# A decoder layer on one core: two streams of matrix work paced by VectorE's load, probabilities scaled on ScalarE, block loads spread, and 24 low parts subtracted by accumulating DMAs

## The chip, the core and the metric

The kernel runs on one core of a Trainium2 chip. The metric is device time in microseconds (us) of one launch; lower is better. TensorE (PE) multiplies, VectorE (DVE), ScalarE (ACT) and GpSimd (POOL) do element work, SyncE (SP) issues transfers, and 16 DMA engines carry them. Each engine works through its own list of instructions in order.

## The reference

One decoder layer on 256 tokens of width 2048, all in fp32: three gated branches, merged by sigmoid gates, an output projection and a LayerNorm.

```python
q_a, k_a, v_a, z_a, u_g, v_g, z_g, q_c, z_c, g_logit = split(x @ w_in)     # 9 x 1024 and 3 x 2048 channels
y_a = causal_attention(q_a, k_a, v_a) * silu(z_a)        # 8 heads of 128; 256 tokens are one block
y_g = spatial_gating(u_g, v_g) * silu(z_g)               # gelu, LayerNorm of v, 128x128 causal mixing, 8 groups
y_c = attention(q_c, mem @ w_mem_k, mem @ w_mem_v) * silu(z_c)   # 4 heads of 256, 256 memory tokens
merged = g0 * (y_a @ w_branch_attn) + g1 * (y_g @ w_branch_sgu) + g2 * (y_c @ w_branch_mem)   # g = sigmoid(g_logit)
out = layer_norm(alpha * x + merged @ w_out)
```

## The kernel before, in words

**Products in parts.** Each fp32 operand is cut into a high part `hi`, the value rounded by a ScalarE copy, and a low part `lo = v - hi`, a VectorE subtraction (`split`, lines 58 to 60). A product is three passes on TensorE: hi by hi, hi by lo, lo by hi.

**Two streams.** TensorE works on two lists of steps that are woven into each other.
- A *c-step* (`classic`) uses one half, 128x1024, of a weight chunk of 1 MB. `load_chunk` loads a chunk into `raw` (two buffers, a third early on), `prep_half` splits a half into `hi` and `lo` (three buffers each, so a new half takes the buffers of the half three before it), two halves ahead of the one in use. Most c-steps make a tile of 128 channels, with 8 matmuls of 512 columns (line 187) and 8 of 256 (line 188); those of a branch projection have 12 of 512 (lines 719 to 721). The chunks in order: memory values 0 to 7 (`mv`), memory keys 8 to 15 (`mk`), `zc` 16 to 23, `qc` 24 to 31, `za` 32 to 34, memory branch 35 to 42, `za` 43 to 47, `qk` 48 to 63 (queries and keys of the attention, which runs beside them), `ug` 64 to 66, attention branch 67 to 74, `ug` 75 to 79, `zg` 80 to 87 (with the mixing of branch B beside it), gating branch 88 to 95, output 96 to 111.
- An *s-step* (`s_stream`) is one half of a product of a Strassen-Winograd scheme with 7 products in a unit; 8 units make 112 steps. Six units make the gate logits, two make `v_a` and `v_g`. A step has 12 matmuls of 512 columns (lines 391 to 393). It needs the parts `sh` (ScalarE) and `sl` (VectorE) of a 128x2048 block, four buffers for both kinds, which the memory tokens `memhl0` to `memhl3` occupy until the memory keys are done. For 64 steps VectorE first subtracts two blocks (lines 309 and 322). The blocks `b0` to `b3` (B11, B12, B22, B21) are loaded by `s_load` into the buffers `rA` and `rB`; sums of x (`xf`) are made early, stored in DRAM and loaded again.

**The order.** The c-steps and s-steps are written out in one order, s-steps at an even rate (`C_STEPS`, `LEAD`, `TAIL` at the end of the code). A scheduler then orders each engine's instructions by its own estimate of when they are ready. All DMAs are issued by SP, in order; `tc.issue_after` chains the early loads so that one is issued after the other has landed, and `riders` are loads tied behind a chunk's load.

**Attention.** Line 594 (attention over tokens, 16 times) and line 534 (over the memory, 8 times) multiply a block of exponentials by the reciprocals of their sums, on VectorE.

Of the kernel before, what the change touches and what calls it, by code (L numbers as in the profile page):

```python
# [27 lines left out]
def decoder_layer(ctx, tc, xT, memT, x_tok, w_st, w_mv, w_mk, w_zc, w_qc, w_za, w_qk, w_ug, w_zg,  # L28
# [63 lines left out]

    def load_chunk(i):

        if 0 < i < 16:
            with tc.issue_after(loaded[i - 1].ins):
                load_one(i)
        else:
            load_one(i)
        for fn in riders.pop(i, ()):  # L100
            with tc.issue_after(loaded[i].ins):
                fn()
# [30 lines left out]
    def prep_half():  # L133
        i, h = divmod(ptr["half"], 2)
        ptr["half"] += 1
        if i in held_at:
            hi, lo = held_at[i](h)
            split(hi, lo, raw[i][:, h].rearrange("p (k c) -> p k c", c=S))
        else:
            hi = wts.tile([P, 1024], F32R, tag="hi", name=f"hi{i}_{h}", bufs=3)  # L140
            lo = wts.tile([P, 1024], F32R, tag="lo", name=f"lo{i}_{h}", bufs=3)
            n = 512 if i == 0 else 1024
            for c in range(0, 1024, n):
                split(hi[:, c:c + n], lo[:, c:c + n], raw[i][:, h, c:c + n])
# [100 lines left out]
    def x_stages():  # L245

        X, F = {}, {}

        def load(g):
            def go():  # L250
                X[g] = wts.tile([P, 2, 4, S], F32, tag="rB", name=f"X{g}", bufs=4)
                nc.sync.dma_start(X[g], xT_v[g])
            return go

        def parts(g, f):
            return lambda: split(xhl_v[g][:, f, :, 0:S], xhl_v[g][:, f, :, S:2 * S], X[g][:, f])

        def sums(g):
            def go():
                F[g] = wts.tile([P, 4, 4, P], F32, tag="rA", name=f"F{g}", bufs=2)  # L260
                a11, a12 = (X[g][:, f, :, 0:P] for f in range(2))
                a21, a22 = (X[g][:, f, :, P:S] for f in range(2))
                s1, s2, s3, s4 = (F[g][:, i] for i in range(4))
                nc.vector.tensor_tensor(s1, a21, a22, op=ALU.add)
                nc.vector.tensor_tensor(s2, s1, a11, op=ALU.subtract)
                nc.vector.tensor_tensor(s3, a11, a21, op=ALU.subtract)
                nc.vector.tensor_tensor(s4, a12, s2, op=ALU.subtract)
            return go

        def sum_parts(g, i):  # L270
            def go():
                t = wts.tile([P, 4, 2 * P], F32R, tag="xsf", name=f"xw{g}{i}", bufs=3)
                split(t[:, :, 0:P], t[:, :, P:2 * P], F[g][:, i])
                late.append(lambda: nc.sync.dma_start(xf_d[i + 1, g], t.bitcast(F32)))
            return go

        return ([load(0), load(1)], [fn for g in range(2) for fn in
                                     [parts(g, 0), parts(g, 1), sums(g)] + [sum_parts(g, i) for i in range(4)]])
# [32 lines left out]
    def s_prep(s):  # L311
# [22 lines left out]
            s_load(u + 1, B11, h)  # L334
        elif p == "M2":
            s_load(u + 1, B22, h)

    def snap(name):
        return work.tile([P, 512], F32, tag="snap", name=name, bufs=5)

    def s_stream(finish):

# [117 lines left out]
            step(go)  # L460
            yield

    riders[5], riders[6] = [x_loads[0]], [x_loads[1]]
    for _ in run(mem_values()):
        pass
    for i, _ in enumerate(run(mem_keys())):
        if x_work:
            x_work.pop(0)()
        if i in (2, 4):
            with tc.issue_after(loaded[ptr["load"] - 1].ins):  # L470
                s_load(0, B12, i // 2 - 1)
        if i in (10, 12):
            for blk in (B11, B22):
                with tc.issue_after(loaded[ptr["load"] - 1].ins):
                    s_load(0, blk, i // 2 - 5)
# [31 lines left out]
    def mem_head(h, q):  # L507
        st = {}

        def fetch():  # L510
            st["k"] = w2(f"mkh{h}", (P, 2, S))
            st["v"] = w2(f"mvh{h}", (P, 2, S))
            for kk in range(2):
                nc.sync.dma_start(st["k"][:, kk], mk_d[2 * h + kk])
            for t in range(2):
                nc.sync.dma_start(st["v"][:, t], mv_d[t, h // 2][:, (h % 2) * S:(h % 2 + 1) * S])

        def scores():
# [13 lines left out]
            nc.vector.reciprocal(sm, sm)  # L532
            for t in range(2):
                nc.vector.tensor_scalar(p[:, t], p[:, t], sm[:, t:t + 1], None, op0=ALU.mult)
            st["p"] = p

        def transposes():
            ps = new_aux(f"mpt{h}", (P, 2, S))
            for mi in range(2):
                for t in range(2):  # L540
                    nc.tensor.transpose(ps[:, mi, t * P:(t + 1) * P], st["p"][:, t, mi * P:(mi + 1) * P], ident)
            st["pt"] = w2(f"mptT{h}", (P, 2, S))
            nc.scalar.activation(st["pt"], ps, AF.Copy)
# [32 lines left out]
    def moba_head(h, q, k):  # L576
        st = {}

        def scores():
# [11 lines left out]
                                     accum_out=sm[:, i:i + 1])  # L591
            nc.vector.reciprocal(sm, sm)
            for i, sl in enumerate((slice(0, P), slice(P, 384))):
                nc.vector.tensor_scalar(p[:, sl], p[:, sl], sm[:, i:i + 1], None, op0=ALU.mult)
            st["p"] = p
            st["v"], st["z"] = w1(f"vah{h}", (P, 2, P)), w1(f"sza{h}")
            for t in range(2):
# [181 lines left out]
        yield from gating()  # L779
        yield from gated_branch(1, 2)  # L780

    C_STEPS, S_STEPS = 160, 14 * UNITS
    LEAD, TAIL = 5, 11
    cs, ss = classic(), s_stream(s_finish)
    done_c = done_s = 0
    for _ in run(cs):
        done_c += 1
        while done_s < S_STEPS and done_s * (C_STEPS - LEAD - TAIL) < (done_c - LEAD) * S_STEPS:
            step(lambda: next(ss))
            done_s += 1  # L790
    flush()


# [129 lines left out]
```

## Time and profile before

| | |
|---|---|
| median of 3 runs | 1005.45 us (1003.4 to 1006.7) |
| profiled execution | 1006.0 us |
| its span, first to last instruction | 1004.3 us |
| granted clock, mean over the span | 0.994 of full speed |
| TensorE idle in the span | 24.8 us |

The page gives the busy time of each engine, then groups of instructions; the trace behind it gives the same for any stretch. The stages stand at these times: memory values to 55 us, memory keys to 99, `zc` and the first s-steps from there, `qk` with the attention 426 to 594, the attention branch 650 to 725, `zg` with the mixing 763 to 846, the gating branch 846 to 901.

### The profile page before, as it was taken

Reading aid. Unit: us, or ns where it says so; the run is one execution under the profiler, and the core shown is the slowest. Engines: PE = TensorE matmul, PEld = TensorE weight load, DVE = VectorE, ACT = ScalarE, POOL = GpSimd, SP = SyncE. Lnnn points to the kernel's source line nnn. Section 1 sums busy time; section 2 is a strip of 40 time slices with the busy share of each in tenths; the row PEclk is TensorE's granted clock in tenths of the full one; section 3 lists DMA queues with packets and bytes.
Section 4 is the critical chain, followed back from the end, with each engine's and each line's share of the span. In section 5 each row is a group of like instructions: output and inputs, shape, how many; then the busy total and the mean of one; then the engine's idle time right before and its main releaser. Section 6 shows DMA issues by size and latency. Waiting matters only on the chain.

```text
span 1004.3 us, 12911 instructions
## 1 busy us (share of the span) xinstructions
PE 979.5 (98%) x4888; PEld 824.4 (82%) x4888; DVE 819.6 (82%) x800; ACT 590.5 (59%) x647; POOL 13.2 (1%) x17
## 2 busy tenths in 40 slices
PE   9999899999999999999999999998999999999995
PEld 7788788888888888888888888876888888878885
DVE  5875986698769987978998898889998989676647
ACT  5744555565586556556566557696566558445520
POOL 0000000000000000000000000000000002000000
PEclk9999999999999999999999999999999999999998
DMA  8899578946896599379548945995899477668622
GB/s 322 315 365 419 217 252 308 338 141 228 316 333 222 218 390 354 132 288 373 219 147 312 359 150 207 340 343 186 303 371 372 143 293 256 247 234 319 227 83 84
DMA packets 68125, 269.28 MB, mean 268 GB/s; under 512 B 7520, under 2 KB 21600, under 8 KB 45536
## 3 DMA queue, kind: packets, MB, share of 16 engines
q1 hardware_dynamic: 68064, 268.47, 72.5%
q8 instruction: 38, 0.62, 0.2%
q14 instruction: 23, 0.19, 0.0%
HBM read 245.37 MB, written 23.07 MB: 267 GB/s over the span
## 4 chain that ended last, share of the span: by engine, by line
PE 79%; DVE 9%; DMA 6%; issue 3%; ACT 3%; SPq 0%; DVEq 0%; ACTq 0%
PE sM L391 8%; PE sM L392 8%; PE sM L393 8%; PE za L187 3%; PE k L187 3%; PE q L187 3%; PE zg L187 3%; PE qc L187 3%; PE mk L187 3%; PE mv L429 3%; PE o L806 3%; PE o L807 3%; PE o L805 3%; PE zc L187 3%; PE b L720 2%
## 5 line engine op out<-in xcount | busy, mean ns | idle before, releaser
L59 ACT ACTIVATE hi<-raw 128x1024 fp32r<-128x1024 f32 (+1 forms) x218 | 228.3, 1050 | 220.7 <-PE b L721 35.5
L60 DVE TENSOR_TENSOR lo<-raw,hi 128x1024 fp32r<-128x1024 f32 (+1 forms) x218 | 262.4, 1209 | 77.4 <-ACT hi L59 73.6
L60 DVE TENSOR_TENSOR sl<-b,sh 128x2048 fp32r<-128x2048 f32 x112 | 255.7, 2285 | 48.3 <-ACT sh L59 48.1
L59 ACT ACTIVATE sh<-b 128x2048 fp32r<-128x2048 f32 x112 | 214.3, 1913 | 85.1 <-PE sM L392 79.6
L309 DVE TENSOR_TENSOR b<-b,b 128x2048 f32<-128x2048 f32 x48 | 109.5, 2283 | 15.3 <-DMA b<-in_w_st_dram 15.3
L391 PE MATMUL sM<-sh,xf 128*128 128x512 f32 x256 | 100.8, 394 | 2.8 <-ACT sh L59 2.8
L392 PE MATMUL sM<-sl,xf 128*128 128x512 f32 x256 | 100.7, 393 | 2.6 <-DVE sl L60 2.6
L393 PE MATMUL sM<-sh,xf 128*128 128x512 f32 x256 | 100.6, 393 | 0.0
L391 PE MATMUL sM<-sh,xhl 128*128 128x512 f32 x192 | 76.4, 398 | 1.6 <-ACT sh L59 1.6
L720 PE MATMUL b<-lo,yhl 128*128 128x512 f32 x192 | 75.6, 394 | 1.8 <-DVE lo L60 1.6
L393 PE MATMUL sM<-sh,xhl 128*128 128x512 f32 x192 | 75.9, 395 | 0.0
L392 PE MATMUL sM<-sl,xhl 128*128 128x512 f32 x192 | 75.8, 395 | 0.0
L721 PE MATMUL b<-hi,yhl 128*128 128x512 f32 x192 | 73.7, 390 | 0.0
L719 PE MATMUL b<-hi,yhl 128*128 128x512 f32 x192 | 73.3, 394 | 0.3 <-ACT hi L59 0.2
L391 PEld LDWEIGHTS sM<-sh,xf 128*128 128x128 f32 x256 | 48.1, 188 | 13.8 <-ACT sh L59 3.3
L392 PEld LDWEIGHTS sM<-sl,xf 128*128 128x128 f32 x256 | 48.2, 188 | 12.6 <-DVE sl L60 3.0
L393 PEld LDWEIGHTS sM<-sh,xf 128*128 128x128 f32 x256 | 48.1, 188 | 10.1
L187 PE MATMUL k<-xhl,hi 128*128 128x512 f32 x128 | 46.8, 403 | 0.0
L187 PE MATMUL za<-xhl,hi 128*128 128x512 f32 x128 | 46.2, 400 | 0.0
L187 PE MATMUL q<-xhl,hi 128*128 128x512 f32 x128 | 46.2, 399 | 0.0
L187 PE MATMUL ug<-xhl,hi 128*128 128x512 f32 x128 | 45.9, 398 | 0.2 <-ACT hi L59 0.2
L187 PE MATMUL zc<-xhl,hi 128*128 128x512 f32 x128 | 45.6, 399 | 0.5 <-ACT hi L59 0.4
(297 smaller groups left out, 1889.8 us busy)
## 6 DMA issues: line engine op xcount, KB each, us to landing
b<-in_w_st_dram SPq DMA_DIRECT2D x64, 1024.0 KB, 7.3
xf<-xf SPq DMA_DIRECT2D x64, 512.0 KB, 5.6
raw<-in_w_br_dram SPq DMA_DIRECT2D x24, 1024.0 KB, 6.5
raw<-in_w_qk_dram SPq DMA_DIRECT2D x16, 1024.0 KB, 7.1
raw<-in_w_o_dram SPq DMA_DIRECT2D x16, 1024.0 KB, 4.8
raw<-in_w_mk_dram SPq DMA_DIRECT2D x8, 1024.0 KB, 9.9
raw<-in_w_zc_dram SPq DMA_DIRECT2D x8, 1024.0 KB, 7.1
raw<-in_w_qc_dram SPq DMA_DIRECT2D x8, 1024.0 KB, 6.6
```

The source lines that it names most:

```text
L59: nc.scalar.activation(hi, v, AF.Copy)
L60: nc.vector.tensor_tensor(lo, v, hi.bitcast(F32), op=ALU.subtract)
L187: nc.tensor.matmul(ps, hi, x, start=first, stop=False)
L309: nc.vector.tensor_tensor(o, rt[u, other, h], o, op=ALU.subtract)
L391: nc.tensor.matmul(ps, ah, hi[:, c], start=first, stop=False, skip_group_check=True)
L392: nc.tensor.matmul(ps, ah, lo[:, c], start=False, stop=False, skip_group_check=True)
L393: nc.tensor.matmul(ps, al, hi[:, c], start=False, stop=last, skip_group_check=True)
L429: nc.tensor.matmul(ps[t][n], lhs, rhs[:, n * 512:(n + 1) * 512], start=(k == 0 and rhs is hi and lhs is xh[t]), stop=(k == KT - 1 and lhs ...
L719: nc.tensor.matmul(ps[t], yh, hi[:, c], start=(k == 0), stop=False)
L720: nc.tensor.matmul(ps[t], yh, lo[:, c], start=False, stop=False)
L721: nc.tensor.matmul(ps[t], yl, hi[:, c], start=False, stop=(k == 7))
L805: nc.tensor.matmul(ps[:, 0:n], mh, hi, start=first, stop=False)
```

## The change

1. The even rate of the s-steps is replaced by a plan (`pace`): each kind of c-step has a cost in VectorE time, an s-step costs 3.2, and s-steps are put where the running sum leaves room, with due times by which a unit's results must stand. The s-steps in the stretch of each kind of chunk go, from before to after: `zc` 9 to 11, `qc` 12 to 8, `za` 5 to 6, memory branch 11 to 12, `za` 8 to 8, `qk` 26 to 32, `ug` 3 to 6, attention branch 15.0 to 14.8, `ug` 7 to 6, `zg` 13 to 8, gating branch 3 to 0.
2. The scaling of the probabilities goes from VectorE to ScalarE (24 instructions).
3. For the second half of the chunks 48 to 63 and 80 to 87, 24 halves, the low part is no longer a VectorE subtraction: ScalarE writes -hi into `lo` and GpSimd issues a DMA that adds `raw` to it (128x1024, 512 KB).
4. The first blocks' loads are spread over earlier chunks as riders, the sums of x move from `rA` to the buffers `snap`, and the chain of loads runs to chunk 19 instead of 15.

```diff
+            if h == 1 and i in by_dma:
+                nc.scalar.activation(lo, raw[i][:, h], AF.Copy, scale=-1.0)
+                nc.gpsimd.dma_start(lo.bitcast(F32), raw[i][:, h], accum_op=ALU.add)
+                nc.scalar.activation(hi, raw[i][:, h], AF.Copy)
+            else:
+                for c in range(0, 1024, n):
+                    split(hi[:, c:c + n], lo[:, c:c + n], raw[i][:, h, c:c + n])
...
+    by_dma = list(range(len(chunks), len(chunks) + 16))
     chunks += [w_qk[j] for j in range(16)]
...
+    by_dma += list(range(len(chunks), len(chunks) + 8))
     chunks += [w_zg[j] for j in range(8)]
...
-                F[g] = wts.tile([P, 4, 4, P], F32, tag="rA", name=f"F{g}", bufs=2)
+                F[g] = [snap(f"F{g}{i}", (P, 4, P)) for i in range(4)]
...
-    riders[5], riders[6] = [x_loads[0]], [x_loads[1]]
+    riders.update({4: [x_loads[0]], 5: [first(B12, 0)], 6: [x_loads[1]], 7: [first(B12, 1)],
+                   10: [first(B11, 0)], 12: [first(B11, 1)]})
...
-                nc.vector.tensor_scalar(p[:, t], p[:, t], sm[:, t:t + 1], None, op0=ALU.mult)
+                nc.scalar.activation(p[:, t], p[:, t], AF.Copy, scale=sm[:, t:t + 1])
...
-        while done_s < S_STEPS and done_s * (C_STEPS - LEAD - TAIL) < (done_c - LEAD) * S_STEPS:
+        for _ in range(plan[i] if i < len(plan) else 0):
```

ScalarE between the memory keys and `zc`, before. `sh0` and `sh1` are the high parts of the first two s-steps, `hi16` those of the first `zc` chunk, `mk7l` and `zc0l` copies of finished tiles:

```order
L59 ACTIVATE hi16_0_865<-raw16_723 128x1024
L59 ACTIVATE hi16_1_890<-raw16_723 128x1024
L59 ACTIVATE sh0_917<-b0_0_0_775 128x2048
L207 ACTIVATE mk7l_914<-mk7_864 128x256
L207 ACTIVATE zc0l_1060<-zc0_994 128x256
L59 ACTIVATE sh1_921<-b0_0_1_833 128x2048
```

The same place after:

```order
L62 ACTIVATE sh0_923<-b0_0_0_418 128x2048
L62 ACTIVATE hi16_0_869<-raw16_730 128x1024
L62 ACTIVATE hi16_1_894<-raw16_730 128x1024
L62 ACTIVATE sh1_927<-b0_0_1_505 128x2048
L218 ACTIVATE mk7l_920<-mk7_868 128x256
L62 ACTIVATE hi17_0_1001<-raw17_843 128x1024
L62 ACTIVATE sh2_1135<-b0_0_0_418 128x2048
L62 ACTIVATE hi17_1_1022<-raw17_843 128x1024
L218 ACTIVATE zc0l_1066<-zc0_1000 128x256
```

`sh1` stood behind `zc0l`, which waits for the first `zc` tile; it and `sh2` now stand ahead of it.

SP beside the end of the memory values, before (`X1` is the second half of x, `xw` are sums of x on their way to DRAM, `b` a block):

```order
L252 DMA X1_266<-in_xT_dram 128x2x1024
L120 DMA mraw7_303<-in_memT_dram 128x512
L122 DMA raw7_302<-in_w_mv_dram 128x2048
L122 DMA raw8_340<-in_w_mk_dram 128x2048
L274 DMA xf1_0_97<-xw00_576 128x1024
```

and after:

```order
L263 DMA X1_268<-in_xT_dram 128x2x1024
L123 DMA mraw7_305<-in_memT_dram 128x512
L125 DMA raw7_304<-in_w_mv_dram 128x2048
L306 DMA b1_0_1_308<-in_w_st_dram 128x2048
L285 DMA xf1_0_97<-xw00_585 128x1024
L285 DMA xf2_0_99<-xw01_614 128x1024
L285 DMA xf3_0_101<-xw02_641 128x1024
L125 DMA raw8_344<-in_w_mk_dram 128x2048
```

A block's load and three stores now stand ahead of the load of chunk 8.

ScalarE near the end of `qk`, where chunk 62 is prepared, before:

```order
L59 ACTIVATE hi62_0_4800<-raw62_4637 128x1024
L207 ACTIVATE q6l_4770<-q6_4687 128x256
L59 ACTIVATE sh68_4764<-b3_4_0_4442 128x2048
L59 ACTIVATE hi62_1_4820<-raw62_4637 128x1024
L606 ACTIVATE ptT4_4682<-pt4_4678 128x384
L59 ACTIVATE hi63_0_4872<-raw63_4730 128x1024
```

and after:

```order
L62 ACTIVATE hi62_0_4955<-raw62_4794 128x1024
L611 ACTIVATE ptT4_4838<-pt4_4834 128x384
L150 ACTIVATE hi62_1_4998<-raw62_4794 128x1024
L62 ACTIVATE sh74_4881<-b0_5_0_4470 128x2048
L148 ACTIVATE lo62_1_4999<-raw62_4794 128x1024
L62 ACTIVATE hi63_0_5054<-raw63_4890 128x1024
```

`lo62_1`, on VectorE's list before, is now a ScalarE copy, here with `sh74` between it and its high part; the accumulating DMA on GpSimd's list waits for it.

## Rows read from the trace of the kernel before

**Rows 1.** The page's first part: busy us of each engine, share, instructions.

```profile
PE 979.5 (98%) x4888; PEld 824.4 (82%) x4888; DVE 819.6 (82%) x800; ACT 590.5 (59%) x647; POOL 13.2 (1%) x17
```

**Rows 2.** Stretches: length; busy PE, PEld, DVE, ACT, POOL; clock, DMA share, GB/s.

```profile
40.00:55.00 15.00, 13.51 (x60) 10.73 (x59) 15.00 (x20) 9.70 (x12) 0.00 (x0) 1.00 0.85 287
55.00:99.30 44.30, 44.30 (x258) 38.73 (x257) 25.25 (x28) 22.17 (x27) 0.00 (x0) 1.00 1.02 412
99.30:126.00 26.70, 23.47 (x111) 19.08 (x110) 24.88 (x15) 14.34 (x14) 0.00 (x0) 0.94 0.60 223
426.00:594.00 168.00, 168.00 (x875) 142.95 (x874) 143.54 (x140) 99.55 (x119) 0.00 (x0) 1.00 0.73 271
650.00:725.00 75.00, 70.15 (x310) 55.79 (x308) 69.99 (x70) 53.53 (x53) 0.00 (x0) 1.00 0.77 278
762.60:846.00 83.40, 83.40 (x437) 71.11 (x436) 76.07 (x71) 55.70 (x57) 10.13 (x7) 1.00 0.70 259
846.00:901.40 55.40, 53.98 (x253) 44.29 (x252) 40.32 (x52) 28.93 (x38) 1.57 (x1) 1.00 0.67 238
```

**Rows 3.** Waits, 650 to 725 us: total us, times, longest.

```profile
PE sM L392 <- DVE sl L60: 2.6, 1, 2.6
```

**Rows 4.** Timeline 104 to 116 us: start, length, [idle before <-releaser].

```profile
104.47 0.40 PE L187 MATMUL zc<-xhl,hi 128*128 128x512 f32 x1
104.82 0.39 PE L391 MATMUL sM<-sh,xhl 128*128 128x512 f32 x1
...
105.02 0.38 ACT L207 ACTIVATE zc0l<-zc 128x256 f32<-128x256 f32 x1 [5.16 <-PE zc L188]
105.30 1.91 ACT L59 ACTIVATE sh<-b 128x2048 fp32r<-128x2048 f32 x1
...
108.84 1.89 ACT L59 ACTIVATE sh<-b 128x2048 fp32r<-128x2048 f32 x1
...
110.79 0.50 PE L391 MATMUL sM<-sh,xf 128*128 128x512 f32 x1 [2.83 <-ACT sh L59]
...
111.82 0.57 PE L392 MATMUL sM<-sl,xhl 128*128 128x512 f32 x1
...
115.17 0.45 PE L392 MATMUL sM<-sl,xf 128*128 128x512 f32 x1
```

**Rows 5.** Groups by line and shape: count, busy us, mean ns, idle before.

```profile
L60 DVE TENSOR_TENSOR lo<-raw,hi 128x1024 fp32r<-128x1024 f32 x214 | 259.7, 1219 | 74.6 <-ACT hi L59 70.8 <-PE sM L392 2.5 <-PE q L188 0.3
L60 DVE TENSOR_TENSOR sl<-b,sh 128x2048 fp32r<-128x2048 f32 x112 | 255.7, 2285 | 48.3 <-ACT sh L59 48.1
L59 ACT ACTIVATE hi<-raw 128x1024 fp32r<-128x1024 f32 x214 | 225.8, 1058 | 217.9 <-PE b L721 35.5 <-PE o L807 30.8 <-PE zc L187 14.7
L59 ACT ACTIVATE sh<-b 128x2048 fp32r<-128x2048 f32 x112 | 214.3, 1913 | 85.1 <-PE sM L392 79.6 <-DVE b L309 3.3 <-DMA raw<-in_w_za_dram 1.5
L309 DVE TENSOR_TENSOR b<-b,b 128x2048 f32<-128x2048 f32 x48 | 109.5, 2283 | 15.3 <-DMA b<-in_w_st_dram 15.3
L594 DVE TENSOR_SCALAR p<-p,sm 128x256 f32<-128x256 f32 x8 | 2.8, 347 | 0.0
L711 ACT ACT_TABLE_LOAD x9 | 11.5, 1283 | 3.2 <-DMA sg<-gl 3.1
```

**Rows 6.** DMA issues: count, KB each, median us from issue to landing.

```profile
xf<-xf SPq DMA_DIRECT2D x64, 512.0 KB, 5.6
raw<-in_w_qk_dram SPq DMA_DIRECT2D x16, 1024.0 KB, 7.1
raw<-in_w_mk_dram SPq DMA_DIRECT2D x8, 1024.0 KB, 9.9
raw<-in_w_zg_dram SPq DMA_DIRECT2D x7, 1024.0 KB, 6.5
```

**Rows 7.** GpSimd in the `zg` stretch, from the timeline.

```profile
777.65 2.42 POOL L664 TENSOR_SCALAR_AFFINE_SELECT ws<-ws 128x128 f32<-128x128 f32 x1 [10.70 <-ACT hi L59]
784.94 0.29 POOL L664 TENSOR_SCALAR_AFFINE_SELECT ws<-ws 128x128 f32<-128x128 f32 x1 [4.87 <-DMA ws<-in_w_sT_dram]
```

More of the change, by code (lines that the diff above doesn't have):

```diff
@@ L43, in w2, with snap @@
         return work.tile(list(shape), F32, tag="w2", name=name, bufs=6)
+    def snap(name, shape=(P, 512)):
+        return work.tile(list(shape), F32, tag="snap", name=name, bufs=5)
     def spill(name, shape, dt=F32):
@@ L93, in load_chunk @@
     def load_chunk(i):
-        if 0 < i < 16:
+        if 0 < i < 20:
             with tc.issue_after(loaded[i - 1].ins):
@@ L142, in prep_half @@
             n = 512 if i == 0 else 1024
-            for c in range(0, 1024, n):
-                split(hi[:, c:c + n], lo[:, c:c + n], raw[i][:, h, c:c + n])
+            if h == 1 and i in by_dma:
[5 more added lines that the diff above has]
+                    split(hi[:, c:c + n], lo[:, c:c + n], raw[i][:, h, c:c + n])
             ready.append((hi, lo))
@@ L259, in go @@
             def go():
-                F[g] = wts.tile([P, 4, 4, P], F32, tag="rA", name=f"F{g}", bufs=2)
+                F[g] = [snap(f"F{g}{i}", (P, 4, P)) for i in range(4)]
                 a11, a12 = (X[g][:, f, :, 0:P] for f in range(2))
                 a21, a22 = (X[g][:, f, :, P:S] for f in range(2))
-                s1, s2, s3, s4 = (F[g][:, i] for i in range(4))
+                s1, s2, s3, s4 = F[g]
                 nc.vector.tensor_tensor(s1, a21, a22, op=ALU.add)
@@ L272, in go @@
                 t = wts.tile([P, 4, 2 * P], F32R, tag="xsf", name=f"xw{g}{i}", bufs=3)
-                split(t[:, :, 0:P], t[:, :, P:2 * P], F[g][:, i])
+                split(t[:, :, 0:P], t[:, :, P:2 * P], F[g][i])
                 late.append(lambda: nc.sync.dma_start(xf_d[i + 1, g], t.bitcast(F32)))
@@ L336, in s_prep @@
             s_load(u + 1, B22, h)
-    def snap(name):
-        return work.tile([P, 512], F32, tag="snap", name=name, bufs=5)
     def s_stream(finish):
@@ L461, in run @@
             yield
-    riders[5], riders[6] = [x_loads[0]], [x_loads[1]]
+    first = lambda blk, h: lambda: s_load(0, blk, h)
+    riders.update({4: [x_loads[0]], 5: [first(B12, 0)], 6: [x_loads[1]], 7: [first(B12, 1)],
+                   10: [first(B11, 0)], 12: [first(B11, 1)]})
     for _ in run(mem_values()):
@@ L468, in decoder_layer @@
             x_work.pop(0)()
[L469 to L475, printed above, removed]
+        if i in (12, 14):
+            riders[ptr["load"]] = [first(B22, i // 2 - 6)]
     while x_work:
@@ L593, in scores @@
             for i, sl in enumerate((slice(0, P), slice(P, 384))):
-                nc.vector.tensor_scalar(p[:, sl], p[:, sl], sm[:, i:i + 1], None, op0=ALU.mult)
+                nc.scalar.activation(p[:, sl], p[:, sl], AF.Copy, scale=sm[:, i:i + 1])
             st["p"] = p
@@ L780, in classic, with pace @@
         yield from gated_branch(1, 2)
-    C_STEPS, S_STEPS = 160, 14 * UNITS
-    LEAD, TAIL = 5, 11
+    S_STEPS = 14 * UNITS
+    KINDS = ([(16, 1.2), (16, 1.75), (6, 1.2), (16, 1.3), (10, 1.2), (32, 1.15), (6, 1.2), (16, 1.6), (10, 1.2),
+              (16, 1.7), (16, 1.9)])
+    C_COST = [cost for n, cost in KINDS for _ in range(n)]
+    DUE = {38: 14, 46: 28, 64: 42, 102: 56, 110: 70, 126: 84, 144: 98, 152: 112}
+    S_COST = 3.2
+    def pace(share):
+        plan, busy, time, s = [], 0.0, 0.0, 0
+        for i, cost in enumerate(C_COST):
+            busy, time, n = busy + cost, time + 2.35, 0
+            lag = max(busy - share * time, -2.0)
+            busy = share * time + lag
+            while i >= 4 and s < S_STEPS and n < 2 and (busy + S_COST <= share * (time + 2.25) or
+                                                        any(i + 3 >= at and s < due for at, due in DUE.items())):
+                busy, time, s, n = busy + S_COST, time + 2.25, s + 1, n + 1
+            plan.append(n)
+        return plan, s
+    share = 0.80
+    while pace(share)[1] < S_STEPS or sum(pace(share)[0][:148]) < S_STEPS:
+        share += 0.005
+    plan = pace(share)[0]
     cs, ss = classic(), s_stream(s_finish)
-    done_c = done_s = 0
-    for _ in run(cs):
-        done_c += 1
-        while done_s < S_STEPS and done_s * (C_STEPS - LEAD - TAIL) < (done_c - LEAD) * S_STEPS:
+    for i, _ in enumerate(run(cs)):
+        for _ in range(plan[i] if i < len(plan) else 0):
             step(lambda: next(ss))
-            done_s += 1
     flush()
```

## The prediction, made before the changed kernel ran

> **What bounds the kernel now.** I read the page's busy times first. TensorE works 979.5 us, VectorE 819.6, ScalarE 590.5 [rows 1]. With 24.8 us of idle time TensorE is the bound: a change that takes nothing from its list can win little more than that, plus what slow matmuls cost. So the next question is where TensorE idles, and the busy time by stretch tells it [rows 2]. At the end of the memory values, 40 to 55 us, it loses 1.5 us, and VectorE is busy without a break. From 99.3 to 126, where the first s-steps start, it loses 3.2 and the clock is 0.94. In the attention branch, 650 to 725, it loses 4.9, VectorE being busy 69.99 of 75. In the gating branch, 846 to 901, it loses 1.4. The rest lies at the program's two ends. In `qk` (168.00 of 168) and in `zg` (83.40 of 83.40) it loses nothing. The reader is to see that the largest single edit, the 24 low parts, falls in the two stretches where TensorE waits for nobody. The waits show who holds it in the attention branch: a low part on VectorE, 2.6 us at once [rows 3]. The timeline shows the start: `sh1` is late, because ScalarE's list has `zc0l` ahead of it, and that waits 5.16 us for the first `zc` tile [rows 4].
>
> **What leaves VectorE.** 24 low parts at 1.219 are 29.3 us, and 24 scalings at 0.347 or somewhat less (the narrow ones are half as wide) about 8, together 37 of 819.6 [rows 1, 5]. Where they leave, they free nothing that TensorE waited for. They pay only through the plan: `qk` takes about 6 s-steps more, so `zg` takes 5 and the gating branch 3 fewer. But neither had much to win (0 and 1.4 us of idle), and the attention branch, which did wait for VectorE, keeps its 15 steps and its own low parts. I take 0 for this; the bounds are 0 and −6.3 (all that these two branches lose).
>
> ScalarE gets 24 more copies at 1.058, 25.4 us, and about 10 for the scalings. In `qk` it is busy 99.55 of 168, and with six more s-steps (six `sh` at 1.913) the sum stays near three quarters of a stretch that grows by 16 us. TensorE's work hides this; without the cover a late copy would cost up to its own microsecond.
>
> **T1, the first s-steps.** Before, TensorE waits 2.83 us for `sh1` and comes back slow: eight matmuls from 111.82 to 115.17, 3.35 us [rows 4]. The usual spacing is 44.30 / (129 + 129/2) = 0.23 for 512 columns, since half the 258 matmuls of the memory keys have 256 [rows 2]. The eight lose 3.35 − 8 x 0.23 = 1.5. At 0.42 each they ran near half speed, the lower level of 1.2 GHz, after the engine had idled; the stretch's granted clock of 0.94 agrees. Together 4.3 us. Afterwards `sh1` is ahead of `zc0l`, and the order puts the first s-step directly behind the memory keys. Its `sh0` gets a buffer when the first half of the last key chunk is done, one half (44.30 / 16 = 2.8 us) before the end. 1.91 for `sh0` and 2.28 for `sl0` end 1.4 after that end; a matmul on either side of the change of stream covers 0.46. So 0.9 is the new wait. For the second step VectorE has `sl0`, two low parts of `zc`, a block subtraction and `sl1` in a row: 2.28 + 2.44 + 2.28 + 2.28 = 9.3, ending 8.4 after the end of the keys; it is wanted at 0.9 + 2.8 + 5.6 = 9.3. It fits with 0.9 to spare. T1 = −4.3 + 0.9 = −3.4, bounds −4.3 and 0.
>
> **T2, the memory values.** SP now has a block of 1 MB and three stores ahead of chunk 8. The stretch moved 287 GB/s where the next one moves 412 [rows 2]: room for 15 x 125 KB/us = 1.9 MB. The two blocks come out of the memory keys, so those are relieved. x comes a chunk earlier, which spreads VectorE's work of that stretch. Bounds −1.5 (its whole idle time) and +2.5 (1 MB at 412 GB/s in series); I take a third of the gain, −0.5, since VectorE had no gap there.
>
> **T3, the attention branch.** ScalarE changes its function table 10 times between chunks 67 and 74 in the old order and 5 times in the new, 1.283 each [rows 5]. The scaling on ScalarE joins the exponentials without a change. ScalarE is not the late one here (53.53 of 75), so of 6.4 us I take 1.0: T3 = −1.0, bounds 0 and −4.9.
>
> **T4, the accumulating DMAs.** The trace has none. What counts is the lead: the time from the last use of the old low part in a buffer to the first use of the new. ScalarE's two copies take 2.1 of it, the transfer D the rest. I counted TensorE's list between the two and priced it at 0.23 and 0.115. Chunk 84: 28 matmuls of 512, 16 of 256 and four small mixing ones, 8.8 us; chunk 85 the same; chunk 48: 8.6; chunk 62: 8.8. There `sh74` stands between the two copies; the high part starts 0.6 earlier, so the copies end 3.4 after the buffer is free. Next come 87 (10.0), 86 (11.1), 49 (11.3), 56, 63 and 80 (11.4), 50 (11.5), 55 (11.8), the others 12.1 to 17.8. D is bounded below by the 512 KB loads, 5.6, and above by 1 MB in a crowded queue, 9.9; a DMA that reads two times 512 KB is nearest to the 1 MB loads of these stretches, 6.5 in `zg` and 7.1 in `qk` [rows 6]. I take 6.5: all leads hold but chunk 62's, 6.5 + 3.4 − 8.8 = 1.1. At 5.6 that is 0.2. At 7.1 it is 0.6 + 1.7 + 0.4 + 0.4 = 3.1. At 9.9 twelve are late and the sum is 20.4.
> The raw buffer is held through the DMA as well: load 6.5, high part 1.06, copies 2.1, DMA 6.5 make 16.2 for a buffer, against about 17.4 in which TensorE does two `zg` chunks (four halves at 2.8, two s-steps at 2.7, mixing). That fits by 1.2. Behind the held load on SP stand the next `xf` loads, wanted two s-steps later (about 11 us against 5.6), and blocks. On GpSimd the accumulates wait behind the affine selects of the mixing weights, ahead of chunks 82, 84 and 86.
>
> The Trainium skill, page "DMA: Bandwidth & Descriptors", section "Anatomy of one DMA — SWDGE (gpsimd) path", gives about 2.0 us plus bytes at 436 GB/s, by which 1 MB would take an estimated 4.4; no accumulate would be late and the sum below would end 1.1 lower. No run so far shows such a transfer.
>
> **Sum.** On the profiled execution (1006.0, of which the span is 1004.3): −3.4 − 0.5 − 1.0 + 1.1 = −3.8, so 1002.2. The profiled run stands 0.6 over the median 1005.45; on the median the forecast is 1001.6.
>
> **Rival 1, the accumulates come late (slower).** Place: TensorE before a `lo` matmul of chunks 48, 62, 84 to 87. The gains, T1 to T3, are 4.9, so within the 0.3% (3 us) that a measurement can tell from no change, it decides from T4 = 7.9, at D = 8.2. GpSimd may be held up: the same affine select took 0.29 and 2.42 us, with VectorE busy nearly throughout [rows 2, 7]. Such a hold-up before each DMA gives D = 8.9 and T4 = 11.3; with 9.9 it is 20.4; halfway, 9.4, about 15, and 1005.45 − 4.9 + 15 = 1015.5. Against it: the sources lie on the chip, and DMA shares are 0.73 and 0.70.
> The Trainium skill, page "SBUF — State Buffer", section "SBUF: two separate sides", states that VectorE and GpSimd share a port pair as an exclusive lock. A VectorE operation with two inputs there shuts out only a GpSimd operation that reads the memory too, and only VectorE's two-port modes keep GpSimd from writing a DMA's descriptors. The affine select's extra 2.1 us agrees with the first half. By the second, the subtractions here wouldn't hold up the accumulates and the sum stays; if they do, it is this rival.
>
> **Rival 2, the relief reaches TensorE.** If all waits behind VectorE and ScalarE go, 1.5 + 4.9 + 1.4 and the start's 3.2 + 1.5 leave: −12.5, 993. For it: VectorE is the releaser in the attention branch, and 37 us less work lets it run ahead before it gets there. Against: leads are capped by three `lo` buffers and four for `sh` and `sl`, so it can't store an advance; and that stretch keeps its load.
>
> **Rival 3, the start gains nothing.** The `zc` stretch has VectorE busy 24.88 of 26.70 already, and takes two s-steps more; if the 0.9 to spare is not there, VectorE sets the pace and T1 is 0. With T2 0 and T3, T4 as above this is 1005.5.
>
> **How the numbers follow.** Forecast 0.42, own range 997 to 1006 (T1 to T4 at nearer bounds); of it faster 0.25, same 0.15, slower 0.02. Rival 1 0.25, between 1007 and 1021; same 0.03, slower 0.22. Rival 2 0.21, all faster. Rival 3 0.12; same 0.10, slower 0.02. That makes faster 0.46, same 0.28, slower 0.26. The range reaches into rival 2 to 991 and into rival 1 to 1017, leaving some 0.06 below and 0.09 above.
>
> **What would show it.** T1: no wait of 5 us on ScalarE before the first `zc` copy, full clock from 99 to 126, a wait near 0.9 for `sl0`. T3: TensorE's wait for VectorE in the attention branch stays at 3 to 5 us. T4: the landing time of the GpSimd DMAs near 6.5 and one wait of TensorE, at chunk 62; `qk` and `zg` else full. Landing times over 8.2, or many waits for a DMA at `lo` matmuls, make the forecast wrong; so does a new wait behind ScalarE in `qk`, or an attention branch that closes its gap.

## The result and the profile after

The changed kernel takes 1015.04 us (median of 4 runs, 1012.25 to 1017.34) against 1005.06 for the kernel before (4 runs): a ratio of 1.0103, 95% interval 1.0083 to 1.0122. It is 10 us slower. The forecast was 1001.6; the time came out where Rival 1 had it (1015.5).

The profiled execution is the fastest of the four (1012.25, span 1010.5), so its trace shows some 6 of the 10 us. The first part of its page, then what the page says of the new DMAs (queue: packets, MB, share of 16 engines; issues: count, KB each, median us to landing):

```profile
PE 979.4 (97%) x4888; PEld 822.7 (81%) x4888; DVE 788.9 (78%) x752; ACT 617.5 (61%) x695; POOL 28.0 (3%) x41
...
q0 software_dynamic: 3456, 12.58, 6.5%
...
lo<-raw POOLq DMA_DIRECT2D x24, 512.0 KB, 7.4
raw<-in_w_mk_dram SPq DMA_DIRECT2D x8, 1024.0 KB, 9.4
```

VectorE lost 31 us of busy time, where the prediction took 37 off its list, and TensorE has the same work as before [rows 1]. The stretches of the same stages (columns as in [rows 2]): end of the memory values, first s-steps, `qk`, attention branch, `ug`, `zg`, gating branch.

```profile
35.00:55.00 20.00, 17.23 (x74) 13.29 (x73) 17.29 (x21) 11.72 (x15) 0.00 (x0) 1.00 1.01 383
99.80:126.00 26.20, 26.20 (x138) 22.32 (x137) 26.20 (x18) 16.55 (x18) 0.00 (x0) 1.00 0.52 201
421.00:610.00 189.00, 185.19 (x947) 156.24 (x946) 146.28 (x123) 129.23 (x153) 12.83 (x15) 1.00 0.94 304
646.70:733.20 86.50, 85.25 (x380) 70.30 (x378) 82.40 (x71) 58.99 (x60) 0.00 (x0) 1.00 0.81 309
733.20:781.00 47.80, 46.17 (x236) 38.22 (x234) 46.90 (x43) 29.88 (x30) 0.25 (x1) 1.00 0.71 242
781.00:860.40 79.40, 72.46 (x381) 60.98 (x380) 43.45 (x55) 51.70 (x61) 12.13 (x15) 0.98 0.87 253
860.40:907.30 46.90, 45.61 (x214) 36.80 (x213) 33.04 (x45) 27.07 (x35) 0.28 (x1) 1.00 0.79 285
```

Read length minus PE. The first s-steps lost 3.2 us before and nothing now; the attention branch 4.9 before and 1.3 now. `qk` and `zg`, which had no idle time at all [rows 2], now lose 3.8 and 6.9. In `zg` VectorE is busy 43 of 79 us: it is not short of VectorE. The waits of TensorE name who came last (total us, times, longest):

```profile
PE zg L199 <- DMA lo<-raw: 4.7, 3, 2.9
PE q L199 <- DMA lo<-raw: 3.2, 3, 1.5
PE zg L198 <- ACT hi L62: 2.3, 2, 1.8
...
PE mk L198 <- ACT hi L62: 1.6, 1, 1.6
...
PE mk L199 <- DVE lo L63: 0.8, 1, 0.8
```

Six of the 24 accumulating DMAs land after TensorE wants them, 7.9 us in sum. The two waits in the memory keys (`mk`) are new too, and make up most of the 2.8 us that the first row above loses: chunk 8 comes late behind the block and the stores that now stand ahead of it. Its load takes 10.9 us from issue to landing, and took 6.0 before. One late accumulate in the timeline, the first:

```profile
417.94 0.99 POOL L149 DMA_DIRECT2D lo<-raw  x1 [415.76 <-DVE za L219]
...
423.76 0.28 PE L199 MATMUL q<-xhl,lo 128*128 128x256 f32 x1
423.88 0.40 PE L198 MATMUL q<-xhl,hi 128*128 128x512 f32 x1
425.28 0.39 PE L199 MATMUL q<-xhl,lo 128*128 128x256 f32 x1 [1.00 <-DMA lo<-raw]
```

It landed 7.3 us after its issue; TensorE stood with the old half done and the new low part not there. The longest of the six waits, 2.9 us at chunk 84, came about in another way:

```profile
816.95 1.06 ACT L62 ACTIVATE hi<-raw 128x1024 fp32r<-128x1024 f32 x1 [1.21 <-DMA raw<-in_w_zg_dram]
...
819.17 1.04 ACT L148 ACTIVATE lo<-raw 128x1024 fp32r<-128x1024 f32 x1
820.13 1.83 POOL L669 TENSOR_SCALAR_AFFINE_SELECT ws<-ws 128x128 f32<-128x128 f32 x1 [8.14 <-DMA ws<-in_w_sT_dram]
821.90 0.85 POOL L149 DMA_DIRECT2D lo<-raw  x1
...
824.50 0.40 PE L198 MATMUL zg<-xhl,hi 128*128 128x512 f32 x1
824.85 0.40 PE L198 MATMUL zg<-xhl,hi 128*128 128x512 f32 x1
825.46 0.47 PE L399 MATMUL sM<-sh,xhl 128*128 128x512 f32 x1
828.82 0.58 PE L199 MATMUL zg<-xhl,lo 128*128 128x256 f32 x1 [2.89 <-DMA lo<-raw]
829.20 0.63 PE L198 MATMUL zg<-xhl,hi 128*128 128x512 f32 x1
829.84 0.63 PE L198 MATMUL zg<-xhl,hi 128*128 128x512 f32 x1
```

```profile
828.80:832.20 3.40, 3.38 (x12) 2.96 (x13) 1.97 (x6) 2.94 (x4) 0.85 (x1) 0.55 0.71 207
```

This DMA landed 6.9 us after its issue, sooner than the median. But ScalarE waited for the chunk itself, and an affine select stood ahead of the DMA on GpSimd, so that it was issued 1.7 us after the copy (0.3 to 0.4 at the 23 others). And TensorE came back slow: a matmul of 512 columns with one of 256 takes 0.64 us from start to start, where it took 0.35 before the wait. The granted clock from 828.8 to 832.2 is 0.55, near the lower level of 1.2 GHz.

### The profile page after: what moved, and what is told of

Same layout as the page of the kernel before. It is cut to its first block, busy times and chain, and to the rows that moved or that the text cites. A ratio compares the mean times of both kernels' runs of the same rounds, so it can differ in the third digit from the quotient of the medians.

```text
span 1010.5 us, 12998 instructions
## 1 busy us (share of the span) xinstructions
PE 979.4 (97%) x4888; PEld 822.7 (81%) x4888; DVE 788.9 (78%) x752; ACT 617.5 (61%) x695; POOL 28.0 (3%) x41
## 4 chain that ended last, share of the span: by engine, by line
PE 66%; DMA 12%; issue 9%; DVE 8%; ACT 4%; SPq 0%; DVEq 0%; ACTq 0%; POOLq 0%; POOL 0%
PE sM L400 7%; PE sM L399 7%; PE sM L401 7%; DMA lo<-raw 5%; PE b L726 3%; PE zc L198 3%; PE mk L198 3%; PE qc L198 3%; PE b L725 3%; PE za L198 3%; PE o L832 3%; PE b L724 3%; PE o L833 3%; PE o L831 3%; PE mv L437 3%
## 5 line engine op out<-in xcount | busy, mean ns | idle before, releaser
L63 DVE TENSOR_TENSOR lo<-raw,hi 128x1024 fp32r<-128x1024 f32 (+1 forms) x194 | 233.6, 1212 | 94.1 <-ACT hi L62 93.4
L62 ACT ACTIVATE hi<-raw 128x1024 fp32r<-128x1024 f32 (+1 forms) x194 | 202.0, 1046 | 142.0 <-PE o L833 29.9
L400 PE MATMUL sM<-sl,xf 128*128 128x512 f32 x256 | 100.8, 394 | 0.1
L400 PEld LDWEIGHTS sM<-sl,xf 128*128 128x128 f32 x256 | 48.1, 188 | 10.5 <-DVE sl L63 0.8
L198 PE MATMUL zg<-xhl,hi 128*128 128x512 f32 x128 | 47.2, 405 | 2.3 <-ACT hi L62 2.3
L198 PE MATMUL mk<-memhl,hi 128*128 128x512 f32 x128 | 45.4, 399 | 1.6 <-ACT hi L62 1.6
```

Of the source, the lines that this page charges most:

```text
L198: nc.tensor.matmul(ps, hi, x, start=first, stop=False)
L400: nc.tensor.matmul(ps, ah, lo[:, c], start=False, stop=False, skip_group_check=True)
```

## The experiments

Each ratio is to the kernel before, run beside it on the same chip.

### The accumulates taken out, in whole, in part, and as plain copies

```diff
-            if h == 1 and i in by_dma:
+            if False:
```

> The changed kernel without the accumulating DMAs: all 24 low parts are VectorE subtractions again; the plan, the scaling on ScalarE and the spread loads stay. Theory A (the accumulates land late and hold the raw buffers; TensorE loses some 5 us in qk and 9 in zg to it): those losses go, little comes in their place, since VectorE would then be busy some 166 of 185 us in qk and 53 of 75 in zg; time 999 to 1003, the median of the changed kernel (1015) less 12 to 16. Rival B (the plan overloads VectorE in qk and the accumulates only cover that): qk shows new waits of TensorE for VectorE of 5 us or more, time 1007 or more. Rival C (the start and the attention branch gained only because of the accumulates' relief): their gains of 6 and 5 us shrink.

Measured: 999.63 us, ratio 0.9961 (0.9944 to 0.9979). The accumulates cost 14 to 15 us (1.0103 / 0.9961, or the medians); without them the other parts win 4. `qk` (176.00 of 176) and `zg` (74.80 of 74.80) are full again. So A holds, B doesn't: VectorE is busy 156.53 of 176 in `qk` and no wait comes of it. Of C something holds: the attention branch loses 3.7 again.

```profile
422.00:598.00 176.00, 176.00 (x912) 149.92 (x911) 156.53 (x136) 110.11 (x132) 0.00 (x0) 1.00 0.71 263
634.30:724.70 90.40, 86.75 (x378) 70.77 (x377) 83.99 (x77) 65.48 (x68) 0.00 (x0) 0.98 0.77 290
...
775.50:850.30 74.80, 74.80 (x403) 64.29 (x402) 61.82 (x69) 55.66 (x64) 11.22 (x8) 1.00 0.73 256
```

Only `qk` (the line that adds the `zg` chunks to `by_dma` removed):

> The changed kernel with accumulating DMAs only for chunks 48 to 63 (16 halves), none in zg. Theory A: the 9 us of zg go, the 5 us of qk stay: 1004 to 1008. Rival B: zg was no VectorE problem, so 1010 or more would need another cause.

Measured: 1001.43, ratio 0.9956 (0.9933 to 0.9978), no slower than without any. `qk` loses 3.5 by its stretch, and the attention branch loses 1.2 instead of 3.7; by which way the relief of VectorE gets there, the run doesn't show. So in `qk` the accumulates cost about what they give. The expectation (1004 to 1008) had missed the second half.

Only `zg` (`by_dma` empty for `qk`):

> The changed kernel with accumulating DMAs only for chunks 80 to 87 (8 halves), none in qk. Theory A: the 5 us of qk go, the 9 us of zg stay: 1008 to 1012, slower than the one with qk alone although it has half as many DMAs. Rival B: qk waits for VectorE instead, 1013 or more.

Measured: 1011.23, ratio 1.0064 (1.0042 to 1.0086). Eight DMAs in `zg` cost 11.6 us more than none, sixteen in `qk` 2.

```diff
-                nc.gpsimd.dma_start(lo.bitcast(F32), raw[i][:, h], accum_op=ALU.add)
+                nc.gpsimd.dma_start(lo.bitcast(F32), raw[i][:, h])
```

> The changed kernel with the 24 GpSimd DMAs writing raw over lo instead of adding it (the low part then holds the whole value, so the output is another one); same bytes written, same waits, same queue, no read of the old contents. If the adding makes the DMA slow (it reads two sources; its 12.6 MB took 6.5% of 16 engines' span, 12 GB/s an engine where the loads got 23): landing falls from a median of 7.4 to 5 or 6 and the time to 1005 to 1009. If the queue and the other loads make it late: landing stays near 7 and the time at 1012 to 1016.

Measured: 1001.2, ratio 0.9960 (0.9944 to 0.9976). This is the cleanest of the runs, since every engine's order is row for row that of the changed kernel: leaving out the addition alone (the low part then holds the whole value) gives back 14 us. The view of the line that issues them (min/median/max ns on GpSimd, then us to landing), first in the changed kernel, then in this one:

```profile
L149 POOL DMA_DIRECT2D lo<-raw x24: 841/854/993, 417.9 to 851.5; - x24
DMA to landing us min/median/max: 4.5/7.4/11.0
```

```profile
L149 POOL DMA_DIRECT2D lo<-raw x24: 527/530/670, 417.9 to 841.4; - x24
DMA to landing us min/median/max: 2.8/5.8/9.8
```

Its queue on the page, its stretches `qk` and `zg`, and its waits of TensorE there:

```profile
q0 software_dynamic: 3456, 12.58, 3.1%
```

```profile
421.30:605.30 184.00, 184.00 (x945) 156.10 (x944) 147.03 (x124) 129.82 (x153) 7.96 (x15) 1.00 0.83 311
776.20:849.60 73.40, 70.78 (x382) 59.80 (x380) 43.23 (x54) 51.70 (x61) 10.54 (x15) 1.00 0.81 280
```

```profile
PE zg L199 <- DMA lo<-raw: 1.3, 1, 1.3
PE zg L198 <- ACT hi L62: 1.3, 2, 0.7
```

The addition makes a landing some 1.6 us longer, at the quiet end (4.5 against 2.8) as in the middle (7.4 against 5.8), and doubles the time on the DMA engines: 6.5% of 1010.5 us / 24 = 2.7 us of all 16 for each, against 3.1% of 998.6 / 24 = 1.3. In each of the six that came late, the same DMA is 1.5 to 2.6 us shorter as a copy. The waits for these DMAs go from six to one.

Because the order is the same, the two traces can be laid side by side. `qk` takes 189.0 us against 184.0, `zg` 79.4 against 73.4, the gating branch 46.9 against 45.9, and the stretches between are alike: 12 of the 14 us. In `zg` TensorE's idle time makes 4.3 of the 6.0. The other 1.7 are busy time, most of it the slow matmuls behind the wait at chunk 84; with the copies TensorE waits 1.3 us there, and the granted clock of the stretch stays at 1.00 (0.98 with the additions).

### The other parts alone

Only the block loads spread, on the kernel before (part 4 of the change):

> The kernel before with only the block loads spread (x and the first blocks earlier, the sums of x in other buffers, the load chain to chunk 19); even rate, VectorE scaling, no accumulates. If the start's gain comes from the loads: the 5.7 us of zc go, 1 to 3 us come in the memory keys, which cost them now; 1000 to 1003. If it comes from the plan (the order behind the keys): 1004 to 1007.

Measured: 1002.48, ratio 0.9976 (0.9960 to 0.9991). The first s-steps are full (25.20 of 25.20 us from 100.8), and the two waits in the memory keys are there, 1.6 and 0.8: the start's gain comes from the loads, at that price.

Only the scaling on ScalarE (part 2):

> The kernel before with only the 24 scalings of probabilities on ScalarE. VectorE loses 8 us, nearly all where TensorE doesn't wait: 1003 to 1006; if the attention branch's gain in the changed kernel (7 to 1.5 us of loss) comes from this and its function tables: 999 to 1002.

Measured: 999.92, ratio 0.9966 (0.9951 to 0.9981), with the attention branch at 80.70 of 81.60 us. The smallest edit wins most.

```profile
623.90:705.50 81.60, 80.70 (x357) 66.10 (x356) 75.03 (x63) 65.92 (x69) 0.00 (x0) 1.00 0.80 308
```

Only the plan instead of the even rate (part 1):

> The kernel before with only the plan in place of the even rate. If the plan alone pays (the kernel without accumulates is 5 us faster than the one before): 1000 to 1003, the zc stretch without loss. If it pays only together with the relief of VectorE: new waits for VectorE in qk, 1005 to 1010.

Measured: 1008.01, ratio 1.0041 (1.0027 to 1.0054): alone it loses 4. The time goes in the attention branch and the `ug` chunks behind it (VectorE 103.63 of 110):

```profile
623.00:733.00 110.00, 104.50 (x459) 84.58 (x458) 103.63 (x101) 76.95 (x84) 0.00 (x0) 0.98 0.81 301
733.00:780.00 47.00, 43.70 (x217) 35.86 (x216) 42.12 (x40) 25.30 (x25) 0.00 (x0) 1.00 0.64 237
```

The two that win, together, at the even rate:

> The kernel before with the scaling on ScalarE and the spread loads, at the even rate, without accumulates. If the two gains add (-3.4 and -2.4 per thousand of 1004): 998. If they win the same waits: 1000 to 1002.

Measured: 997.27 (996.68 to 997.40), ratio 0.9928 (0.9911 to 0.9945). The gains add, and this beats both kernels. From here the plan costs 0.9961 / 0.9928, 3 per thousand, and the accumulates 1.0103 / 0.9961, 14.

```profile
620.00:701.50 81.50, 80.58 (x356) 66.04 (x355) 74.92 (x63) 65.91 (x69) 0.00 (x0) 1.00 0.80 308
...
748.90:836.70 87.80, 85.22 (x439) 72.31 (x438) 76.86 (x69) 52.64 (x57) 14.84 (x7) 0.98 0.70 257
```

### How some 2 us more for each becomes 14

Two ways: each accumulate is late against its own lead (L), or it keeps the raw buffer from the next load (R). In the changed kernel's `zg` six of seven loads of a chunk follow a landing within 0.2 us, and SP, which issues them, stands 32.8 us for accumulates there, so R looked strong:

```profile
SPq L125 <- DMA lo<-raw: 32.8, 7, 9.4
```

The plain copies speak against R alone: with them SP still stands 24.5 us and ScalarE waits 9.6 us for chunks of `zg` (10.2 with the additions), yet the stretch loses 2.6 us instead of 6.9.

```diff
-            lo = wts.tile([P, 1024], F32R, tag="lo", name=f"lo{i}_{h}", bufs=3)
+            lo = wts.tile([P, 1024], F32R, tag="lo", name=f"lo{i}_{h}", bufs=4)
...
```

> The changed kernel with four buffers for the low parts instead of three (the buffers w1 go from 8 to 7 and snap from 5 to 4 to make room). ScalarE's copy into a low part then no longer waits for the half three before, so each accumulate has some 3 to 5 us more lead; DMAs, bytes and queue stay. Theory A (the leads were too short for landings of 4.5 to 11 us): the waits for accumulates in qk and zg fall from some 8 us to under 3, time 1002 to 1008. Rival D (what binds is the raw buffer, held until the accumulate has landed, so that the next chunk comes late): the waits move to hi parts behind late loads, time 1010 or more.

Measured: 1011.09, ratio 1.0068 (1.0043 to 1.0093). It gives back 4. The median landing is longer here, 8.4, the waits for accumulates in `zg` are 3.3 instead of 4.7, those in `qk` are gone, and waits for `sl` (5.1 us) come in their place. In between, it settles nothing.

Four of the `zg` chunks, in two choices (`by_dma += [len(chunks) + j for j in (0, 2, 4, 6)]`, then `(0, 1, 4, 5)`):

> The changed kernel with only four accumulating DMAs, for chunks 80, 82, 84 and 86; the two raw buffers alternate, so all four fall on the same one. The kernel without any took 999.6, with all eight of zg 1011.2. Theory R (the raw buffer's cycle: the next load waits until the accumulate has landed; a round of load, copies and accumulate took 18.7 to 21 us where TensorE needs 17.4 for the two chunks): that one buffer still goes round in some 19 us, three or four rounds each 1.5 to 2 us too long, 1004 to 1008. Theory L (each accumulate is late on its own for want of lead: 8.6, 11.6, 11.1 and 8.8 us for copies of 2.1 and a landing near 7): 1.6 us in sum, 1000 to 1002.5.

> The same number of accumulating DMAs, for chunks 80, 81, 84 and 85, so that each raw buffer has one in every other round. Leads are 8.6, 13.8, 11.1 and 9.2 us, near those of the other choice. Theory R: two rounds of one buffer take 19 + 12 us against 2 x 17.4, so the buffers keep up: 999 to 1002, clearly under the even choice. Theory L: the same as the even choice within 1 us.

Measured: 1002.92, ratio 1.0003 (0.9978 to 1.0027), and 1003.78, ratio 0.9991 (0.9973 to 1.0009). No difference that can be told: R's gap of 2 us or more isn't there. Half the DMAs cost about a third of what eight did.

Two more raw buffers in `zg`, with accumulates in `zg` alone and then in the whole change:

```diff
+        elif i in (84, 85):
+            t = wts.tile([P, 2, 1024], F32, tag="rB", name=f"raw{i}", bufs=4)
...
-        return i - 3 if i <= 16 or i >= OUT + 2 else i - 2
+        return i - 3 if i <= 16 or i >= OUT + 2 or 84 <= i <= 87 else i - 2
```

> Accumulating DMAs for all eight chunks of zg and none in qk, as in the run that took 1011.2 (and 999.6 without any), but chunks 84 and 85 are loaded into two buffers that the blocks have left, so no load of 84 and 85 waits for an accumulate, and those of 86 and 87 wait for an older one. Leads, bytes and copies of the accumulates stay about as they were (9 to 16 us). Theory R (load, copies and accumulate go round in a raw buffer in 20 to 27 us where TensorE has 19.5 for two chunks): the loss in zg falls from 10 to under 4 us, 1001 to 1005. Theory L (lateness of each accumulate against its lead): the loss stays, 1008 to 1012.

> The changed kernel (1015) with all 24 accumulates, and chunks 84 and 85 in the two buffers that the blocks have left. Theory R: of the 9.4 us lost in zg 5 or more go, 1006 to 1010. Theory L: 1012 to 1016.

Measured: 1012.70, ratio 1.0068 (1.0034 to 1.0102), and 1013.68, ratio 1.0085 (1.0055 to 1.0114). The `zg` stretch with the closed round (first) and with it opened (second, and its wait for accumulates):

```profile
773.70:859.50 85.80, 78.67 (x405) 65.45 (x404) 51.55 (x58) 57.19 (x65) 14.12 (x15) 0.98 0.83 251
```

```profile
778.30:863.80 85.50, 78.44 (x405) 65.23 (x403) 52.04 (x60) 59.69 (x69) 12.78 (x16) 0.98 0.90 270
```

```profile
PE zg L201 <- DMA lo<-raw: 5.8, 4, 2.8
```

The same 7.1 us lost, with the waits at the accumulates themselves. But the hold isn't gone with the two buffers: SP stands 38.1 us for accumulates in that stretch, 39.3 without them. In the second run the copies did come in time: those for 84 to 87 end 2.0 us after the last use of the old low part, where they end after 3.6 to 6.4 in the changed kernel. Yet the accumulate of chunk 84 is issued 2.7 us after its copy, behind an affine select that itself waited for its data, lands in 10.5, and TensorE waits 5.5 for it. So the held buffer alone is not the answer. In the changed kernel both ways act: what a held load makes late takes a part of the lead, and landing overruns what is left. The runs don't price the two apart.

A third raw buffer in `qk` (the place of `vg` for chunks 50, 53 and 56), no accumulates in `zg`:

> The changed kernel with accumulates in qk alone (that took 1001.4), and a third raw buffer for chunks 50, 53 and 56 (the place of vg, which is empty until branch B), so that chunks 50 to 58 are loaded one chunk earlier. Theory R: TensorE's waits at chunks 50 to 58, some 3.5 of the 6.2 us lost in qk, shrink to 1 or less: 997 to 999.5. Theory L: the leads of the low parts are the same, the waits stay, 1000.5 to 1002.5.

Measured: 1013.38, ratio 1.0096 (1.0064 to 1.0127), 12 us over the same kernel without the buffer. In `qk` TensorE loses 2.7 instead of 3.5; but the first s-steps (23.65 of 25.70, clock 0.94) and the `ug` stretch (50.77 of 57.10) lose again. What links them to that buffer I can't say; the run decides nothing on R.

Accumulates of half the width, VectorE subtracting the rest:

```diff
+                nc.scalar.activation(lo[:, a], raw[i][:, h, a], AF.Copy, scale=-1.0)
+                nc.gpsimd.dma_start(lo[:, a].bitcast(F32), raw[i][:, h, a], accum_op=ALU.add)
+                nc.scalar.activation(hi, raw[i][:, h], AF.Copy)
+                nc.vector.tensor_tensor(lo[:, b], raw[i][:, h, b], hi[:, b].bitcast(F32), op=ALU.subtract)
```

> The changed kernel (1015) with accumulating DMAs of half the width: each of the 24 adds 128x512 (256 KB), and VectorE subtracts the other half of the low part. As many DMAs, the same waits, the same buffers. Theory L (an accumulate is late when landing is longer than its lead; 6 of 24 were, 9.7 us in sum, and raw loads behind them): landing falls from 7.4 to 5 or 6, as with the plain copies, and the time to 1001 to 1006. If the count of DMAs or their issue on GpSimd (0.85 us each) costs: 1010 or more.

Measured: 1014.83, ratio 1.0100 (1.0069 to 1.0131). A miss: landing falls only to 6.5, the waits for accumulates to 4.6 (2.9 in `zg`, 1.7 in `qk`), and the attention branch and `ug` lose 5.8 and 4.3:

```profile
PE b L726 <- ACT yhl L62: 4.3, 1, 4.3
PE zg L201 <- DMA lo<-raw: 2.9, 2, 1.5
PE ug L201 <- DVE lo L63: 2.8, 2, 2.0
...
PE k L201 <- DMA lo<-raw: 1.7, 1, 1.7
```

Eleven halves of `qk` without those that were late:

```diff
-    by_dma = list(range(len(chunks), len(chunks) + 16))
+    by_dma = [len(chunks) + j for j in (1, 3, 4, 5, 6, 7, 8, 9, 11, 12, 13)]
```

> The changed kernel with accumulates for 11 halves of qk alone, those of the chunks 49, 51 to 57 and 59 to 61, without 48, 50 and 58, whose accumulates were late, and 62 and 63; none in zg. With all 16 it took 1001.4, with none 999.6. Theory L: the 4 us that three late accumulates cost in qk go (the leads left are 9.8 to 17.3 us), and VectorE's relief still helps the attention branch: 996 to 999.5. If other accumulates become late in their place (the s-steps move, and landings reach 11 us): 1000 to 1004.

Measured: 1003.01, ratio 0.9989 (0.9973 to 1.0006). In `qk` L's part came true: no wait for an accumulate, 181.57 of 182.20 us. But the attention branch (78.25 of 81.50) and the stretch behind (51.42 of 54.80) lose 6.6, where the kernel with all 16 lost 2.7.

These two and the third raw buffer show a limit of such runs: an edit moves the s-steps that the scheduler puts into the attention branch and `ug`, and TensorE's idle time there ranged from 1 us to 10 over the variants. Only the plain copies left the order alone.

## Why the prediction was wrong

**The step that failed** is T4: "I take 6.5: all leads hold but chunk 62's". Its 1.1 us measured some 14, the difference between the kernel with and without accumulates. Four things were wrong in it.

First the size. The landing time has no one value. In a quiet stretch it was 4.5 us; with block loads on the way it was 10 to 11 (the fourth and fifth of `qk` took 10.7 and 10.3), and the upper bound of 9.9 didn't hold it. The ten accumulates with a block's load on the way beside them took 7.6 to 11.0, the fourteen others 4.5 to 8.7. The plain copies spread as widely (2.8 to 9.8), so the spread is there without the addition, which puts some 1.6 us on top. The traffic rose as well: DMA share in `qk` from 0.73 to 0.94, in `zg` from 0.70 to 0.87.

Second the form of the sum. A wait is what landing exceeds its lead by, so the mean landing says little. With each DMA's own landing the same working gives: chunk 48, 7.3 + 2.1 + 0.3 for its issue − 8.6 = 1.1, chunk 50, 11.0 + 2.4 − 11.5 = 1.9, chunk 80, 10.2 + 2.5 − 11.4 = 1.3. TensorE stood 1.0, 1.5 and 1.3 us there, and 0.7 at chunk 58, which landed in 10.8. Chunk 62, the only one forecast late, wasn't (it landed in 4.6). In these the leads were sound; the one D for all wasn't.

Third, the copies. At chunks 84 and 87, which hold 3.3 of the 7.9 us, landing was near the forecast (6.9 and 6.0). What failed is "ScalarE's two copies take 2.1 of it": with the measured leads, chunk 84 has 3.6 for the copies + 1.7 to the issue + 6.9 − 9.3 = 2.9, and chunk 87 has 5.1 + 0.4 + 6.0 − 11.1 = 0.4. At 84 the copies stood behind the chunk's load, for which ScalarE waited. At 87 they stood behind ScalarE's own list: it had waited 6.3 us for a small load (`sg`) that SP had issued behind a chunk's load held by an accumulate, and then worked without a break up to those copies. "That fits by 1.2" was wrong as well: for chunks 82 to 87 it takes 16.3 to 24.4 us from a load's issue to its accumulate's landing, where 16.2 were taken and about 17.4 were there.

Fourth, 7.9 us of waits at accumulates are only about half of the 14. Beside the plain copies most of the rest shows: 1.3 us of slow matmuls behind the wait at chunk 84, waits for high parts in `zg` of 2.3 instead of 1.3 (the longest, 1.8, behind the same wait for `sg`), 1.0 in the gating branch, and 0.7 for a low part of an s-step in `qk`. Some 2 us lie between the profiled executions and the medians.

**Rival 1** had the time, and half the mechanism. That its 1015.5 stands so near is partly luck: its 15 came from 9.4 us for every landing, and with the median of 7.4 its sum gives 4.3. GpSimd was mostly not held up: it took up 23 of the 24 DMAs within 0.5 us of ScalarE's copy and spent 0.84 to 0.99 on each; once, before chunk 84, an affine select of 1.83 stood ahead, and there the longest wait is. What the Trainium skill, page "SBUF — State Buffer", section "SBUF: two separate sides", says of VectorE's subtractions and descriptors agrees with the 0.84 to 0.99. The estimate from the Trainium skill, page "DMA: Bandwidth & Descriptors", section "Anatomy of one DMA — SWDGE (gpsimd) path", 4.4 us for 1 MB, agrees with the quiet landings of 4.5 and is less than half of the crowded ones.

**T1** was right and too small: −3.4 forecast, and the whole loss went (26.20 of 26.20), with no wait of 0.9. **T2** had the wrong sign: the memory values won about 1 (their wait for a low part went from 1.5 us to 0.4), but the late chunk 8, bounded at +2.5, cost 2.4 in the memory keys. Together the spread loads measured −2.4. **T3** was mis-sized, and its mechanism was wrong: −1.0 forecast, −3.4 by the ratio (−3.9 by the medians) from the scaling alone. In the branch itself 4.9 us of idle time became 0.9. VectorE ended the longest wait there, as I wrote, but I had priced only ScalarE's tables, and these are not it. From the branch's first matmul to its last, ScalarE changes its table 10 times before, 10 times with the scaling alone, and 6 times with the plan alone, where the branch still loses 4.4. VectorE's busy time fell by 5 us over the whole run (819.6 to 814.4), and of the 24 scalings only 4 stood in the branch. What of the gain is VectorE's shorter list and what the new order of the lists the runs don't separate. **The plan**, costed at 0, cost 4 alone and 3 beside the scaling. It takes steps out of `zg`, which had no loss; alone, the attention branch and the `ug` chunks behind it lose 8.8 us, where they lost 5 before. Why they do is not shown.

**Rival 2** was partly there: the attention branch did close its gap, in the changed kernel to 1.3 us. **Rival 3** did not happen.

## What to carry to other kernels

A transfer put into the path of an engine that never waited must be judged by its longest landing, not its median, against each single lead, and by what it holds back itself: here held loads made the copies of later chunks late. The place to put it is where that engine already has slack. A small edit (24 scalings moved, 3 to 4 us won) can be worth more than a large one where nobody waits (24 low parts, a loss). When a change has several parts, time them apart: two of the four parts here made a kernel of 997, and the other two took it to 1015.

## What the runs showed of the hardware

- The same 512 KB moved by GpSimd within the chip's memory took 1.3 us of all 16 DMA engines as a copy and 2.7 as an addition; issue took 0.53 and 0.85 us of GpSimd, landing 2.8 and 4.5 at the least.
- Behind a wait of 2.9 us TensorE's granted clock was 0.55 from 828.8 to 832.2, and its matmuls took 0.64 us a pair instead of 0.35, some 1.3 us more in all. What decides such a drop is not shown: with the scaling alone TensorE stands 2.6 us once in the mixing, and its clock stays at 1.00 there.
- Eight affine selects on GpSimd of one shape took 5.8 us together in the changed kernel, four of them 0.28 or 0.29 each, and 16.3 in the kernel of 997 us, one of them 7.93. VectorE was busy 43 of 79 us of `zg` in the first and 76.86 of 87.80 in the second; that this is the cause is not shown. One of these ends the longest wait that is left in the kernel of 997:

```profile
PE mix L672 <- POOL ws L661: 2.6, 1, 2.6
```
